# A planner of TensorE's order that charges for changes between wide, full and tiled matmuls

## The chip, the cores and the metric

One core of a Trainium2 chip runs the whole kernel. The metric is the device time of one execution in microseconds, median of several runs; the profile is one further execution, of which every instruction is recorded. TensorE (PE) does the matmuls, VectorE (DVE), ScalarE (ACT) and GpSimd (POOL) the rest, and SyncE (SP) issues most of the DMAs.

## What is computed

Two layers of an encoder on 512 tokens of width 1024. Each layer normalises, projects to 3728 columns, runs four token mixers on parts of them, joins them in an output projection, and then routes each of 16 experts to its 64 best tokens. Cut from the reference:

```
for l in range(DEPTH):                                   # DEPTH = 2
    h = rms_norm(x, norm_mix_g[l])
    p = jnp.einsum('bsd,dp->bsp', h, w_in[l])
    fa, fb, fc, fd = jnp.split(p, [A_IN, A_IN + B_IN, A_IN + B_IN + C_IN], axis=-1)
    ya = rwkv7_mixer(fa, ...)            # a scan over the tokens, both ways, 4 heads of 64
    yb = gqa_axial_mixer(fb, ...)        # softmax attention, 4 query heads
    yc = gated_deltanet_mixer(fc, ...)   # chunks of 64 tokens, both ways, 4 heads
    yd = dilated_window_mixer(fd, rel_bias)              # windowed attention, 6 heads
    x = x + jnp.einsum('bsm,md->bsd', jnp.concatenate([ya, yb, yc, yd], -1), w_out[l])
    x = x + expert_choice_ffn(rms_norm(x, norm_ffn_g[l]), ...)   # 16 experts x 64 tokens, 3 weights of 1024x1024 each
return rms_norm(x, norm_final_g)
```

## The kernel before, in words

A layer has two stages. In the **mixers' stage** the projection (L701, and L838 for the output) runs as triples of fp32r matmuls over the full array, 128 rows by 128 columns, 512 wide: a high and a low half of the weights and of the activations. These are the wide matmuls. Mixers A and C work in heads of 64, and so in matmuls on a quarter of the array (64 rows by 64 columns, which the profile writes 64\*64), in a long chain of small steps through TensorE and VectorE: Gram matrices (L1130, L1381), a blockwise inverse (L912, L917), a solve (L942, L960), a scan of 8 chunks (L981, L988 in `scan`), the output (L1016, L1209), a transpose at the end (L1232 for A, L1440 for C). Each runs twice in a layer, for two groups of heads; tiles of A's chain are called cA, those of C's cC. Mixers B (L1493, L1505, L1515) and D (L1560, L1569, L1579) are attention, in matmuls of 64 rows by 128 columns and of 128 rows by 64, with transposes on the full array between. In the **experts' stage** 402 MB of weights in both layers flow through 17 slots of 1 MB on SyncE's queue (L1805), and L1819 multiplies with them, 128 rows by 64 columns. A router, a top-64 on VectorE (L1679, L1680) and a gather come before the first expert.

No engine's order is written by hand. The class `Order` records every instruction as the program is built, groups matmuls that were written one after the other into nodes of up to 700 ns by its own costs, and plans: `forward` is a list scheduler that goes through time, and whenever an engine is free takes the ready node of highest rank; `backward` makes new ranks from the plan. After six rounds (`ROUNDS`) the plan with the earliest end by the planner's own clock is kept, and every engine's order is fixed by it. So a change of TensorE's choices also moves the orders of the other engines. Only TensorE has a chooser of its own, `pick` (L240): it takes the node of highest rank, except that it takes a dense one if little dense work was done in the last `WINDOW`, or a thin one if much was (`LOW`, `HIGH`). A heap's entry is the pair of minus the rank and the number, ranks are in ns, so an entry's first number within 5000 of another's means 5 us of rank. A matmul costs the same there whatever stood before it:

```
i = self.pick(heaps[e], t) if e == "PE" else heapq.heappop(heaps[e])[1]
start[i] = t
end = free[e] = t + nodes[i]["cost"]
```

## Time and profile before

| | us |
|---|---|
| median of 3 runs (2005.76 to 2012.01) | 2007.81 |
| the profiled execution, its own time | 2007.23 |
| its span, first to last instruction | 2005.4 |
| PE busy in the span | 1748.3 (87%) |
| DVE busy | 977.4 (49%) |
| ACT busy, POOL busy | 442.0, 348.1 |
| DMA | 471.95 MB, mean 235 GB/s |

Beside the mean shares the profile has the span cut in stretches: of each engine the time that it was busy there, the clock that TensorE was granted as a share of 2.4 GHz, and the rate of the DMAs. The mixers' stages are about 0 to 509 us and 998 to 1493 us, the experts' 509 to 998 and 1493 to 1985. In the timeline each row has the start, the duration, the engine, the line, what is written from what, the array's rows and columns with the shapes, and after the x how many records were merged. A matmul in plain fp32 leaves two records, one in fp32r or a transpose leaves one. The recorded ends of matmuls are modelled and overlap the next one, so what a matmul costs is read from its start to the next one's start.

### The profile page before, as it was taken

Reading aid. Unit: us, or ns where it says so; the run is one execution under the profiler, and the core shown is the slowest. Engines: PE = TensorE matmul, PEld = TensorE weight load, DVE = VectorE, ACT = ScalarE, POOL = GpSimd, SP = SyncE. Lnnn points to the kernel's source line nnn. Section 1 sums busy time; section 2 is a strip of 40 time slices with the busy share of each in tenths; the row PEclk is TensorE's granted clock in tenths of the full one; section 3 lists DMA queues with packets and bytes.
Section 4 is the critical chain, followed back from the end, with each engine's and each line's share of the span. In section 5 each row is a group of like instructions: output and inputs, shape, how many; then the busy total and the mean of one; then the engine's idle time right before and its main releaser. Section 6 shows DMA issues by size and latency. Waiting matters only on the chain. (4 is left out here: it accounts for less than half of the span.)

```text
span 2005.4 us, 31717 instructions
## 1 busy us (share of the span) xinstructions
PE 1748.3 (87%) x12870; PEld 957.5 (48%) x12870; DVE 977.4 (49%) x2581; ACT 442.0 (22%) x882; POOL 348.1 (17%) x313
## 2 busy tenths in 40 slices
PE   6989999999499988869889999999877998798695
PEld 5766666666233322323267666667652332232232
DVE  5597878667422212222166977785872222221223
ACT  4333343433001000000034333334320000000001
POOL 3452124320100000000054511433101000000000
PEclk9999999999699998989989899999988999999898
DMA  5311111226799999999842111112297999999995
GB/s 143 79 36 28 38 35 38 64 71 261 285 409 409 409 409 408 409 409 409 346 141 66 27 33 35 39 33 88 86 361 297 408 409 409 409 409 409 409 409 239
DMA packets 191797, 471.95 MB, mean 235 GB/s; under 512 B 24411, under 2 KB 82683, under 8 KB 191522
## 3 DMA queue, kind: packets, MB, share of 16 engines
q1 hardware_dynamic: 186037, 457.07, 60.2%
q0 software_dynamic: 2816, 8.53, 1.1%
q10 hardware_dynamic: 2797, 4.32, 0.6%
q8 instruction: 101, 1.65, 0.3%
q14 instruction: 46, 0.38, 0.1%
HBM read 461.40 MB, written 8.48 MB: 234 GB/s over the span
## 5 line engine op out<-in xcount | busy, mean ns | idle before, releaser
L1819 PE MATMUL bd<-we,xh 128*64 128x512 f32 x800 | 210.7, 606 | 33.5 <-DMA we<-in_expert_w_up_dram 33.5
L1819 PE MATMUL cA<-we,xh 128*64 128x512 f32 x768 | 191.6, 596 | 22.7 <-DMA we<-in_expert_w_down_dram 22.7
L487 POOL TENSOR_TENSOR wl<-wr,wh 128x512 fp32r<-128x512 f32 x104 | 143.1, 1377 | 349.2 <-PE pj L701 262.0
L1819 PE MATMUL pj<-we,xh 128*64 128x512 f32 x800 | 203.1, 604 | 0.1
L701 PE MATMUL pj<-hh,wh 128*128 128x512 f32 x336 | 153.6, 457 | 0.0
L487 DVE TENSOR_TENSOR y<-cA,y 128x512 fp32r<-128x512 f32 x32 | 22.1, 692 | 268.5 <-ACT y L1750 268.3
L1819 PEld LDWEIGHTS bd<-we,xh 128*64 128x64 f32 x800 | 64.6, 139 | 161.8 <-issue 105.9
L1708 POOL DMA_INDIRECT xh<-xg,idx x16 | 15.5, 971 | 706.8 <-DVE idx L1705 437.5
L701 PE MATMUL pj<-hh,wl 128*128 128x512 f32 x336 | 133.3, 397 | 0.0
L701 PE MATMUL pj<-hl,wh 128*128 128x512 f32 x336 | 133.2, 397 | 0.0
L1819 PEld LDWEIGHTS cA<-we,xh 128*64 128x64 f32 x768 | 59.5, 137 | 139.2 <-issue 96.7
L1819 PEld LDWEIGHTS pj<-we,xh 128*64 128x64 f32 x800 | 60.2, 138 | 108.4 <-issue 101.8
L504 DVE SCALAR_TENSOR_TENSOR xh<-xh,gate,bd 128x512 f32<-128x512 f32 x32 | 23.9, 747 | 173.5 <-PE bd L1819 171.6
L1819 PE MATMUL bd<-slab,xh 128*64 128x512 f32 x224 | 72.6, 623 | 37.5 <-DMA slab<-in_expert_w_up_dram 37.5
L838 PE MATMUL pj<-slab,b 128*128 128x512 f32 x320 | 98.5, 423 | 3.6 <-DVE xres L487 1.5
L504 DVE SCALAR_TENSOR_TENSOR xh<-xh,pj 128x512 f32<-128x512 f32 x34 | 23.4, 687 | 155.1 <-ACT xh L507 155.1
L507 ACT ACTIVATE xh<-pj 128x512 f32<-128x512 f32 x46 | 27.4, 596 | 308.3 <-PE pj L1819 304.6
L669 ACT CAST wh<-wr 128x512 fp32r<-128x512 f32 x104 | 63.9, 617 | 87.1 <-PE pj L701 40.8
L1819 PE MATMUL cA<-slab,xh 128*64 128x512 f32 x256 | 76.4, 598 | 7.3 <-DMA slab<-in_expert_w_down_dram 7.3
L701 PEld LDWEIGHTS pj<-hh,wh 128*128 128x128 f32 x336 | 64.3, 191 | 31.8 <-issue 18.2
L1750 ACT CAST y<-cA 128x512 fp32r<-128x512 f32 x32 | 18.7, 585 | 247.8 <-PE cA L1819 247.8
L701 PEld LDWEIGHTS pj<-hh,wl 128*128 128x128 f32 x336 | 63.8, 190 | 14.8
(473 smaller groups left out, 3207.5 us busy)
## 6 DMA issues: line engine op xcount, KB each, us to landing
we<-in_expert_w_gate_dram SPq DMA_DIRECT2D x100, 1024.0 KB
we<-in_expert_w_up_dram SPq DMA_DIRECT2D x98, 1024.0 KB
we<-in_expert_w_down_dram SPq DMA_DIRECT2D x96, 1024.0 KB
slab<-in_expert_w_down_dram SPq DMA_DIRECT2D x32, 1024.0 KB
slab<-in_expert_w_up_dram SPq DMA_DIRECT2D x28, 1024.0 KB
slab<-in_expert_w_gate_dram SPq DMA_DIRECT2D x28, 1024.0 KB
wr<-in_w_in_dram SPq DMA_DIRECT2D x96, 256.0 KB
b<-in_w_out_dram SPq DMA_DIRECT2D x20, 256.0 KB
```

What stands on the lines that cost most here:

```text
L487: (eng or self.nc.vector).tensor_tensor(out, a, b, op=op)
L504: (eng or self.nc.vector).scalar_tensor_tensor(out, a, s, b, op0=op0, op1=op1)
L507: self.nc.scalar.activation(out, a, fn, **k)
L669: nc.scalar.copy(hi, w)
L701: self.nc.tensor.matmul(pt[:, sl], a[:, k % 4], b[:, k, sl], start=(k == 0 and i == 0), stop=(k == KC - 1 and i == 2))
L838: nc.tensor.matmul(pt, a, b, start=(i == 0), stop=(i == len(terms) - 1))
L1708: nc.gpsimd.indirect_dma_start(dst, None, src, bass.IndirectOffsetOnAxis(ap=idx, axis=0))
L1750: nc.scalar.copy(yh[:, f], pts[f])
L1819: self.nc.tensor.matmul(pts[f][sl], src[:, kk, sl], w[ei][k][:, 512 * f : 512 * f + 512], start=(kk == 0), stop=(kk == KC - 1))
```

## The change

The planner gets three numbers: `STAY` = 5000, `LONG` = 2600, `TURN` = 160 (ns). `record` gives every matmul a kind: "dense" if its operands are not plain fp32 (the wide ones), "tiled" if it is plain fp32 and uses less than 128 rows or 128 columns, "plain" otherwise (mostly transposes). A node keeps the kind of its first and of its last matmul. `pick` first looks for ready nodes that begin with the kind that TensorE is at, and whose rank is within `STAY` of the best; as long as less than `LONG` was spent in that kind, the best of these is taken, ahead of the old rules for dense and thin work. A node of another kind costs `TURN` more on the planner's clock. No instruction is added or taken away; orders alone change. Below the planner every line number of the changed kernel is 12 higher than before (L701 is L713 there).

```diff
+    STAY, LONG, TURN = 5000.0, 2600.0, 160.0
...
+            kind = "dense" if not f32 else "tiled" if k[1] - k[0] < 128 or o[1] - o[0] < 128 else "plain"
...
             node = last
+            node["out"] = kind
...
+            if eng == "PE":
+                node["in"] = node["out"] = kind
...
-        if done < self.LOW and rate(top) < self.DENSE:
+        alike = [e for e in heap if nodes[e[1]]["in"] == self.state and e[0] < top[0] + self.STAY]
+        if alike and self.stay < self.LONG:
+            top = min(alike)
+        elif done < self.LOW and rate(top) < self.DENSE:
...
-        rec.append((t + nodes[i]["cost"], nodes[i]["work"]))
-        return i
+        turn = 0.0 if nodes[i]["in"] == self.state else self.TURN
+        self.stay = 0.0 if turn else self.stay + nodes[i]["cost"]
+        self.state = nodes[i]["out"]
+        self.turns += turn > 0
+        rec.append((t + turn + nodes[i]["cost"], nodes[i]["work"]))
+        return i, turn
...
-                    i = self.pick(heaps[e], t) if e == "PE" else heapq.heappop(heaps[e])[1]
+                    i, turn = self.pick(heaps[e], t) if e == "PE" else (heapq.heappop(heaps[e])[1], 0.0)
                     start[i] = t
-                    end = free[e] = t + nodes[i]["cost"]
+                    end = free[e] = t + turn + nodes[i]["cost"]
```

Counted over both orders, in the mixers' stages of the two layers: neighbours of different kind fall from 716 to 410. Neighbours of different array shape (128\*128, 64\*64, 128\*64, 64\*128 and a few smaller ones) fall from 698 (347 and 351) to 512 (257 and 255). Of the 716, 177 are between plain and dense, both on the full array; afterwards 101. Changes between one tiled shape and another, which are of one kind for the planner, rise from 163 to 205. In the experts' stages changes of shape fall from 121 to 93.

The first place is TensorE in the first layer, where the solve of A's first group (L942, four blocks of 8) runs between projections (L701) and B's attention. Before:

```order
L1493 MATMUL bd_2776<-xh_2194,xh_2193 128x512
L942 MATMUL cA_969<-g_115_701,ar_566 64x64 x8
L942 MATMUL cA_970<-g_115_701,ar_566 64x64 x8
L942 MATMUL cA_969<-g_115_701,ar_566 64x64 x8
L701 MATMUL pj_2730<-hh_103,wh_2725 128x512
L701 MATMUL pj_2730<-hl_104,wh_2725 128x512
L701 MATMUL pj_2730<-hh_103,wl_2726 128x512
L701 MATMUL pj_2730<-hh_103,wh_2725 128x512
L701 MATMUL pj_2730<-hl_104,wh_2725 128x512
L701 MATMUL pj_2730<-hh_103,wl_2726 128x512
L942 MATMUL cA_970<-g_115_701,ar_566 64x64 x8
L1505 MATMUL bd_2787<-const,ba_2782 128x128 x4
```

and with the change (L942 is L954, L701 is L713, L1493 is L1505):

```order
L1505 MATMUL bd_2776<-xh_2194,xh_2193 128x512
L954 MATMUL cA_969<-g_115_701,ar_566 64x64 x8
L954 MATMUL cA_970<-g_115_701,ar_566 64x64 x8
L954 MATMUL cA_969<-g_115_701,ar_566 64x64 x8
L954 MATMUL cA_970<-g_115_701,ar_566 64x64 x8
L713 MATMUL pj_2644<-hh_103,wh_2633 128x512
L713 MATMUL pj_2644<-hl_104,wh_2633 128x512
L713 MATMUL pj_2644<-hh_103,wl_2634 128x512
L713 MATMUL pj_2644<-hh_103,wh_2633 128x512
L713 MATMUL pj_2644<-hl_104,wh_2633 128x512
L713 MATMUL pj_2644<-hh_103,wl_2634 128x512
```

The solve's four blocks stand together, where a projection stood between the third and the fourth.

The second place is TensorE in the first layer's second scans, of A (cA) and C (cC) at once; L838 is the output projection of the rows of mixers that are ready. Before:

```order
L988 MATMUL cA_3683<-g_624_3313,g_619_3293 64x64
L988 MATMUL cA_3684<-g_624_3313,g_619_3293 64x64
L988 MATMUL cA_3683<-g_624_3313,g_619_3293 64x64
L988 MATMUL cA_3684<-g_624_3313,g_619_3293 64x64
L838 MATMUL pj_5169<-slab_4939,b_945_5165 128x512 x2
L838 MATMUL pj_5169<-slab_4939,ba_5166 128x512
L1569 MATMUL bd_5210<-const,ba_5199 128x128 x2
L981 MATMUL cA_3701<-g_655_3655,g_634_3374 64x64
L981 MATMUL cA_3702<-g_655_3655,g_634_3374 64x64
L981 MATMUL cA_3701<-g_655_3655,g_634_3374 64x64
L981 MATMUL cA_3702<-g_655_3655,g_634_3374 64x64
L988 MATMUL cC_4279<-g_751_4193,g_738_4060 64x64
```

and with the change (L981 is L993, L988 is L1000, L1569 is L1581, L1579 is L1591, L1560 is L1572):

```order
L1000 MATMUL cA_3683<-g_624_3313,g_619_3293 64x64
L1000 MATMUL cA_3684<-g_624_3313,g_619_3293 64x64
L1000 MATMUL cA_3683<-g_624_3313,g_619_3293 64x64
L1000 MATMUL cA_3684<-g_624_3313,g_619_3293 64x64
L1581 MATMUL bd_5252<-const,ba_5241 128x128 x2
L1000 MATMUL cC_4279<-g_751_4193,g_738_4060 64x64
L1000 MATMUL cC_4278<-g_751_4193,g_738_4060 64x64
L1000 MATMUL cC_4279<-g_751_4193,g_738_4060 64x64
L1000 MATMUL cC_4278<-g_751_4193,g_738_4060 64x64
L993 MATMUL cA_3701<-g_655_3655,g_634_3374 64x64
L993 MATMUL cA_3702<-g_655_3655,g_634_3374 64x64
L993 MATMUL cA_3701<-g_655_3655,g_634_3374 64x64
```

Between the first and the last step of these two scans there are 42 matmuls of L838 before in either layer, and none afterwards; they stand ahead of the scans or behind them.

The third place is TensorE at the head of A's first chain in the second layer: four matmuls of L1085 give the decays and rates that A's work on ACT and VectorE starts from. Before:

```order
L1085 MATMUL cA_8150<-xh_7944,lw_8109 128x512
L701 MATMUL pj_9839<-hh_7767,wh_9826 128x512
L701 MATMUL pj_9839<-hl_7768,wh_9826 128x512
L701 MATMUL pj_9839<-hh_7767,wl_9827 128x512
L701 MATMUL pj_9839<-hh_7767,wh_9826 128x512
L701 MATMUL pj_9839<-hl_7768,wh_9826 128x512
L701 MATMUL pj_9839<-hh_7767,wl_9827 128x512
L1085 MATMUL cA_8155<-xh_7944,lw_8109 128x512
L1085 MATMUL cA_8156<-xh_7944,lw_8109 128x512
```

and with the change (L1085 is L1097, L1023 is L1035):

```order
L713 MATMUL bd_9908<-hh_7767,wl_9898 128x512
L1097 MATMUL cA_8150<-xh_7944,lw_8109 128x512
L1097 MATMUL cA_8155<-xh_7944,lw_8109 128x512
L1035 MATMUL pj_9866<-const,b_1826_9864 128x2 x4
L713 MATMUL cC_7824<-hh_7767,g_1498_7776 128x256
L713 MATMUL cC_7824<-hl_7768,g_1498_7776 128x256
L713 MATMUL cC_7824<-hh_7767,g_1499_7777 128x256
L713 MATMUL cC_7824<-hh_7767,g_1498_7776 128x256
L713 MATMUL cC_7824<-hl_7768,g_1498_7776 128x256
```

Before, 9 projection matmuls (L701) stand between the first and the second of the four, 6 between the second and the third, none between the last two. Now it is 18, none and 24.

## Rows read from the trace of the kernel before

**Rows 1.** The page's second part: GB/s that the DMAs moved, in 40 equal slices

```profile
GB/s 143 79 36 28 38 35 38 64 71 261 285 409 409 409 409 408 409 409 409 346 141 66 27 33 35 39 33 88 86 361 297 408 409 409 409 409 409 409 409 239
```

**Rows 2.** Stretches, each stage: us, busy us (instructions) of each engine, granted clock, DMA, GB/s

```profile
0.00:508.90 508.90, 459.27 (x4637) 333.27 (x4637) 369.68 (x1087) 186.95 (x390) 151.01 (x133) 0.96 0.28 84
508.90:998.00 489.10, 413.23 (x1784) 146.31 (x1786) 109.75 (x201) 31.66 (x47) 18.02 (x26) 0.95 0.99 394
998.00:1493.40 495.40, 456.15 (x4645) 328.29 (x4641) 372.27 (x1058) 183.90 (x386) 157.09 (x128) 0.97 0.27 83
```

**Rows 3.** Stretches, the same columns: the mixers' stages without their heads and ends

```profile
50.00:500.00 450.00, 419.42 (x4371) 302.58 (x4370) 336.87 (x983) 162.30 (x344) 133.24 (x111) 0.97 0.24 71
1050.00:1490.00 440.00, 412.53 (x4403) 296.39 (x4401) 338.82 (x986) 163.24 (x348) 131.20 (x110) 0.98 0.24 75
```

**Rows 4.** SyncE's timeline and a stretch: the weights' queue after the mixers of layer one

```profile
548.03 7.29 SPq L1805 DMA_DIRECT2D we<-in_expert_w_gate_dram  x5
...
523.00:545.00 22.00, 13.54 (x49) 5.22 (x51) 3.62 (x10) 1.15 (x1) 5.28 (x9) 0.67 0.37 136
```

**Rows 5.** TensorE's timeline, 418 to 422 us: start us, duration us, what, records

```profile
418.00 0.69 PE L960 MATMUL cC<-g,g 64*64 64x64 f32 x32
418.52 0.30 PE L988 MATMUL cA<-g,g 64*64 64x64 f32 x8
418.64 0.41 PE L960 MATMUL cC<-g,g 64*64 64x64 f32 x16
418.98 0.73 PE L838 MATMUL pj<-slab,b 128*128 128x512 f32 x2
419.55 0.39 PE L838 MATMUL pj<-slab,ba 128*128 128x512 f32 x1
419.78 0.63 PE L838 MATMUL pj<-slab,b 128*128 128x512 f32 x2
...
420.94 0.40 PE L838 MATMUL pj<-slab,ba 128*128 128x512 f32 x1
421.26 0.34 PE L981 MATMUL cA<-g,g 64*64 64x64 f32 x8
421.43 0.41 PE L960 MATMUL cC<-g,g 64*64 64x64 f32 x16
421.77 0.44 PE L1579 MATMUL bd<-ba,dv 128*64 128x128 f32 x4
```

**Rows 6.** TensorE's timeline: transposes on the full array among wide matmuls

```profile
489.06 0.60 PE L636 MATMUL cC<-const,xres 128*128 128x128 f32 x4
489.41 0.95 PE L838 MATMUL pj<-slab,b 128*128 128x512 f32 x3
490.19 0.60 PE L636 MATMUL cA<-const,xres 128*128 128x128 f32 x4
```

**Rows 7.** TensorE's timeline: steps of the second scans in layer one

```profile
427.84 0.34 PE L981 MATMUL cA<-g,g 64*64 64x64 f32 x8
...
430.55 0.34 PE L981 MATMUL cA<-g,g 64*64 64x64 f32 x8
...
450.04 0.28 PE L981 MATMUL cC<-g,g 64*64 64x64 f32 x5
```

**Rows 8.** Stretch, the same columns: the second scans in layer one

```profile
418.00:451.00 33.00, 29.02 (x480) 20.63 (x483) 25.57 (x97) 10.56 (x28) 7.92 (x8) 1.00 0.20 63
```

**Rows 9.** Timeline and a stretch: the head of A's first chain in layer two

```profile
1088.47 1.12 PE L1085 MATMUL cA<-xh,lw 64*128 64x512 f32 x2
...
1094.67 1.13 PE L1085 MATMUL cA<-xh,lw 64*128 64x512 f32 x4
...
1100.00:1150.00 50.00, 43.44 (x362) 31.73 (x360) 49.83 (x148) 18.30 (x34) 26.50 (x21) 0.90 0.12 31
```

**Rows 10.** Stretches: two with the clock that TensorE was granted

```profile
459.00:466.00 7.00, 4.44 (x64) 3.31 (x58) 6.76 (x20) 3.16 (x6) 0.00 (x0) 1.00 0.61 188
462.00:472.00 10.00, 7.24 (x33) 5.22 (x29) 8.86 (x24) 3.08 (x6) 0.00 (x0) 0.83 0.94 322
```

More of the change, by code (lines that the diff above doesn't have):

```diff
@@ L372, in forward @@
         N = len(nodes)
-        self.recent = deque()
+        self.recent, self.state, self.stay, self.turns = deque(), None, 0.0, 0
         need = [len(nd["deps"]) + len(nd["tiles"]) for nd in nodes]
```

## The prediction

> **What bounds the kernel now.** First the rate of the DMAs over the span [rows 1]: near 35 GB/s in most of the mixers' stages, at a flat 409 in the experts' ones. Then the same cut by stages [rows 2]: 508.9 us of mixers with PE busy for 459.3, 489.1 us of experts at 394 GB/s with PE busy for 413.2, and 495.4 us of mixers again with PE busy for 456.2. So the experts' stages belong to the queue of weights, and the mixers' stages to TensorE, most of all in their middle: of 450 us in the first layer PE was busy for 419.4, of 440 in the second for 412.5 [rows 3]. It waited there for 30.6 and 27.5 us, 58 together; DVE comes next with 336.9 and 338.8 us.
>
> A gain in the mixers reaches the end of the kernel. The queue of weights fills its free slots, then stands still until the first experts give slots back: from 523 to 545 us it moved 136 GB/s with PE at work for 13.5 of 22 us, and issues go on at 548 [rows 4]. The first expert starts a fixed chain (router, top 64, gather) after the last matmul of the mixers. If that comes 10 us earlier, so does the stream's second part, as long as the first part is loaded by then, and the 22 us of low rate are the reserve for that. So I pass on what the mixers gain in full, in either layer, and count nothing for the 28 changes of shape that the experts' stages lose: PE waits for weights there.
>
> **What a change costs, from rows.** All in [rows 5], start to start. A wide matmul among its like takes 0.23 us (419.55 to 419.78). The two at 418.98 that follow tiled ones take 0.57, where two would take 0.46: 0.11 more. The wide one at 420.94 that stands before a tiled one takes 0.32: 0.09 more. On the tiled side, 32 records of L960 followed by another 64\*64 group take 0.52, so 16 take 0.26; the 16 at 418.64 that are followed by a wide matmul take 0.34: 0.08 more. There and back is 0.28 us, and the first tiled matmul after the change may add a few hundredths, which these rows don't resolve: 0.14 to 0.17 us a change. I take 0.15.
>
> Two things differ from what the planner charges. **Plain beside dense is free.** Four transposes between triples of wide matmuls take 0.35 us, the triple behind them 0.78 instead of 0.69 [rows 6]: 0.44 for the detour, 0.11 a transpose. If a transpose alone took as long as a quarter of a wide matmul, 0.06, the detour would hold 0.2 us of change, 0.1 each way, and the 76 changes of this kind that go (177 to 101) would save another 7.6 us; nothing in the array's shape changes there, so I take 0 and keep the 7.6 us for the range. **A change between tiled shapes is not free.** The 16 records at 421.43 are followed by L1579 in 128\*64, and take 0.34 [rows 5], as the ones before a wide matmul do. For the planner that is one kind. So shapes are to be counted, not kinds.
>
> The Trainium skill has this as a rule (TensorEngine Tiling (Array Packing), Key Properties): changing the tiling mode, not just the tile, drains the engine. By the rule the sum is one over shapes, as in the row; by the planner's kinds it would be 306 changes and 46 us. The trace sides with the rule against the planner's grouping.
>
> **The sum.** In the mixers 698 changes of shape become 512: 186 less, 90 in the first layer and 96 in the second. At 0.15 us that is 27.9 us less for TensorE, 26 to 32 by the bounds, 39 with the transposes. That is all the change removes; nothing is added, no instruction, no DMA. SyncE's queue keeps its rows, only their places shift with the plan, and the weights' order is fixed by the program. The solve (first place of the order) is a clean case: two changes less, and A's chain gets its fourth block earlier.
>
> **What the longer stays cost.** The second place is where I expect part of the gain to be lost. The second scans have steps of PE, DVE, PE, DVE that can't overlap in one chain. In 418 to 451 us PE was busy for 29.0 of 33 us, DVE for 25.6 [rows 8], and PE was so busy because 42 wide matmuls, 42 x 0.23 = 9.7 us, filled the gaps. They are gone from there. With them go 17 changes of shape, 2.6 us. Of the 31.5 us from the first L988 at 418.52 [rows 5] to the last L981 at 450.04 [rows 7], some 17 us of PE's work stay, with PE's few waits. But the chain has its own pace: a step took 2.71 us where it went fast (427.84 to 430.55, [rows 7]), with DVE serving both chains. Eight steps are 21.7 us. So PE will wait for about 5 us in this scan, and as much in the second layer's, whose order has the same 42 and 0. Bounds: 0, if D's attention and DVE's lighter load let the steps run faster than any seen, and 10 us per layer, if they keep nearly the pace of before (27 of 31.5 us). I take 5, two layers 10.
>
> A wait like this can cost the clock. TensorE was busy for 4.4 of 7 us from 459 to 466, and the mean clock in 462 to 472 is 0.83 [rows 10], that is a third of the stretch at 1.2 instead of 2.4 GHz: some 3.4 us, worth up to 1.7 us of wide matmuls. If each second scan brings one such drop, that is 0 to 3.4 us; it lies in the range and not in the sum.
>
> The third place costs in the second layer only. The four L1085 start within 6.2 us before (1088.47 to 1094.67, [rows 9]); with 42 projection matmuls among them instead of 15 the fourth comes 27 x 0.23 = 6.2 us later, less where the 256-wide ones take half: about 5. Behind it is the one stretch where DVE is the bound, 49.8 of 50 us [rows 9]. DVE can do other work meanwhile; 0 to 5 us, I take 2.
>
> Sum: -27.9 + 10 + 2 = -15.9. From the profiled execution's 2007.2 that gives 1991.3; that execution lies 0.6 below the median, which I leave aside: **1991 us**.
>
> **Rivals.**
>
> *The gain arrives whole, or more.* The planner had a TensorE without changes, so every plan ran late by 698 x 0.15 = 105 us, and the orders of DVE and ACT were made for times that never came. With a price close to the measured one they fit better, and some of the 58 us of waiting goes too. Without losses in the scans: 1979; with 8 us of waiting gone as well: 1971. Against it: the price is put on kinds, so 101 changes are still charged that cost nothing and 205 are not charged that do.
>
> *It gives back what it saves.* Fillers taken out of the second scans cost 20 us by the upper bound above, the head 5, a clock drop in each layer 3: 28 of 28, so 2007. The range of this case is 1999 to 2013.
>
> *Slower: stays ahead of the chains.* A stay may last 2.6 us on the planner's clock while a better-ranked chain matmul waits. A layer goes through two rounds of A and C in series, each some 30 hops from PE to DVE and back; 60 hops a layer, 120 in all. One wide matmul more ahead of each hop, 0.23 us, is 28 us: there it turns. At two it is 28 us slower, 2035. For it: between the first and last step of C's first scan in layer one there are 75 projection matmuls where there were 51, 5.5 us more. Against it: in the three other first scans the count goes 45 to 42, 39 to 45 and 54 to 54, and the inverse and solve stand closer together than before. Range 2013 to 2035.
>
> *The change doesn't do what it says* I can leave out: the order shows it.
>
> **How the numbers follow.** A measurement of this kernel tells about 0.3%, 6 us, from no change: faster is below 2001.8, slower above 2013.8. Part given back, 1983 to 1999: 0.45. Whole or more, 1970 to 1983: 0.17. Given back, 1999 to 2013: 0.20, a quarter of it below 2001.8. Slower: 0.18. So faster 0.45 + 0.17 + 0.05 = 0.67, same 0.15, slower 0.18. The range leaves out 0.05 below 1974 and 0.14 above 2016, so it is 1974 to 2016; the forecast's own is 1983 to 1999.
>
> **What would show it.** PE's busy time in the mixers should fall by about 28 us over both layers, and the first wide matmul after tiled ones be as dear as before, only rarer. In the second scans no L838, a span of 20 to 24 us instead of 31.5, and waits of PE for DVE of some 5 us that weren't there. The stretches at 409 GB/s should be as long as before and start earlier, by about 7 us in the first layer and 16 in the second. The fourth L1085 of layer two should start later after the first. I am wrong if PE's waits in the mixers grow by more than 28 us, if the clock falls in many places, or if the gap in the weights' queue closes before the mixers' gain is spent. The place that decides is the second scan: if its steps take 3.5 us although nothing fills them, the gain is gone.

## The result and the profile with the change

The change makes the kernel slower: 2021.04 us, median of five runs (2015.92 to 2026.88), against 2008.98 for the kernel before beside it. The ratio is 1.0063, 95% interval 1.0045 to 1.0082. The forecast was 1991 us with a range to 2016; the time is outside it, on the other side. The profiled execution of the change took 2015.92 us, the fastest of its five; its span is 2014.1.

The page with the change, the granted clock and the rate of the DMAs in 40 slices (the rate answers [rows 1]):

```profile
PEclk9979999989699998989989799999888999999898
GB/s 147 80 30 18 39 51 38 85 45 186 353 409 409 409 409 409 409 409 409 344 130 74 19 28 40 44 27 96 44 323 351 409 408 409 410 408 410 409 409 239
```

The granted clock of before in the same slices:

```profile
PEclk9999999999699998989989899999988999999898
```

Stretches of the trace with the change, columns as in [rows 2]: the stages, then the mixers without head and end, which answer [rows 3]:

```profile
0.00:509.00 509.00, 449.58 (x4637) 339.48 (x4637) 366.09 (x1087) 187.42 (x390) 148.01 (x133) 0.94 0.25 76
1001.00:1498.00 497.00, 447.65 (x4643) 337.10 (x4639) 362.79 (x1057) 183.61 (x386) 152.10 (x128) 0.94 0.25 74
...
50.00:500.00 450.00, 408.95 (x4355) 307.02 (x4356) 331.22 (x977) 160.90 (x341) 129.58 (x111) 0.94 0.21 61
1050.00:1490.00 440.00, 403.57 (x4352) 303.94 (x4350) 325.38 (x960) 160.88 (x342) 127.17 (x111) 0.95 0.21 62
```

PE's busy time fell by some 10 us in the first layer and 9 in the second, not by 14 each. It waits in the middle of the mixers for 41.1 and 36.4 us instead of 30.6 and 27.5 [rows 3], and its granted clock there is 0.94 and 0.95 instead of 0.97 and 0.98. So each of the two things that should have stayed small grew.

From both traces I took the start of the last router transpose (L1674 of before), of the first expert matmul (L1819) and of the last L1756 of each layer. All later tables use these. "Half clock" is the time at a granted clock of 0.5, "waits" the idle time ahead of matmuls inside the stage, "changes" the neighbours of different array shape in the order. All in us, first layer + second layer:

| | before | with the change |
|---|---|---|
| mixers, to the last L1674 | 508.2 + 488.1 | 508.6 + 489.9 |
| from there to the first L1819 (top 64, gather) | 26.0 + 25.6 | 29.1 + 28.9 |
| experts, to the last L1756 | 470.7 + 469.7 | 470.0 + 470.5 |
| sum | 1988.2 | 1997.0 |
| half clock in the mixers | 38.7 + 30.7 | 57.9 + 60.5 |
| waits in the mixers | 48.3 + 37.9 | 58.4 + 48.2 |
| changes in the mixers | 347 + 351 | 257 + 255 |

The mixers gain nothing although 186 changes are gone, and the gather, which nobody touched, loses 6.4 us. The table holds one execution of each kernel, with the change the fastest of its five: these two differ by 8.7 us, the medians by 12.1.

**The gather.** The weights' queue and the first gather in the first layer, with the change (SyncE's timeline; SyncE's waits from 455 to 500; VectorE's wait for the gathered rows; a stretch that answers [rows 4], and the time of the gather itself):

```profile
471.79 26.51 SPq L1817 DMA_DIRECT2D we<-in_expert_w_gate_dram  x8
...
SPq L1817 <- PE cC L1028: 15.6, 1, 15.6
...
534.47 0.31 DVE L513 TENSOR_SCALAR gate<-gs 64x1 f32<-64x1 f32 x2 [8.79 <-DMA gs<-ag,idx]
...
523.00:545.00 22.00, 10.06 (x39) 4.22 (x41) 3.72 (x10) 1.47 (x2) 3.40 (x7) 0.63 0.71 280
526.00:536.00 10.00, 0.27 (x2) 0.27 (x2) 0.30 (x2) 1.15 (x1) 2.12 (x2) 0.50 1.03 411
```

The same of before, for rows that were not shown:

```profile
SPq L1805 <- PE cC L1016: 1.4, 1, 1.4
...
462.30 0.89 SPq L1805 DMA_DIRECT2D we<-in_expert_w_gate_dram  x2
...
530.98 0.31 DVE L501 TENSOR_SCALAR gate<-gs 64x1 f32<-64x1 f32 x2 [5.72 <-DMA gs<-ag,idx]
526.00:536.00 10.00, 3.75 (x14) 2.19 (x16) 1.68 (x4) 1.15 (x1) 2.11 (x2) 0.50 0.20 57
```

The prefetch waits for C's last output matmul of the layer (L1028, L1016 before), which comes 9.5 us later, so it starts 9.5 us later and still runs at 411 GB/s when the gather starts. The gather waits 3.1 us longer, and everything behind it too.

**The second scans.** Stretches from the first L988 to the last L981 of the second scans, with the change and before ([rows 7] end there), in the first layer also the stretch from there to the last L1674:

```profile
430.10:456.70 26.60, 23.62 (x373) 17.93 (x374) 22.55 (x101) 11.34 (x25) 5.29 (x5) 0.68 0.20 61
456.70:508.60 51.90, 45.15 (x424) 35.15 (x420) 40.69 (x149) 14.02 (x32) 1.09 (x3) 0.97 0.56 212
1417.50:1444.00 26.50, 23.55 (x373) 17.76 (x374) 22.31 (x101) 11.47 (x25) 5.27 (x5) 0.68 0.19 62
```

```profile
418.50:450.10 31.60, 28.08 (x455) 19.83 (x446) 24.95 (x93) 9.81 (x26) 7.76 (x7) 1.00 0.19 61
450.10:508.20 58.10, 50.30 (x437) 37.26 (x431) 44.60 (x170) 19.15 (x44) 1.12 (x3) 0.96 0.72 270
```

No L838 is left, as the order says. But the scan takes 26.6 us, not 20 to 24. PE waits for 3.0 us there, not for more than the 3.5 of before. What is new is the clock: 0.68, which is 17.1 us at 1.2 GHz in a stretch that had full clock before.

The 42 matmuls of L838 all stand ahead of these scans now: between the first and the second scans there are 96 of them in either layer instead of 54, behind the second ones 120 as before. So the second scans start later (11.6 us in the first layer), and the stretch behind them is no longer than before, 51.9 us instead of 58.1.

### The profile page after: what moved, and what is told of

It is laid out like the page before. It is cut to its first block, busy times and chain, and to the rows that moved or that the text cites. A ratio compares the mean times of both kernels' runs of the same rounds, so it can differ in the third digit from the quotient of the medians.

```text
span 2014.1 us, 31694 instructions
## 1 busy us (share of the span) xinstructions
PE 1728.0 (86%) x12870; PEld 975.3 (48%) x12870; DVE 961.8 (48%) x2581; ACT 442.3 (22%) x882; POOL 340.2 (17%) x313
## 4 chain that ended last, share of the span: by engine, by line
PE 48%; DMA 23%; DVE 19%; ACT 2%; issue 2%; POOL 1%; SPq 0%; ACTq 0%; DVEq 0%; POOLq 0%
PE pj L1831 8%; DMA we<-in_expert_w_up_dram 8%; DMA we<-in_expert_w_down_dram 7%; PE bd L1831 7%; PE pj L713 7%; PE cA L1831 6%; PE pj L850 4%; DMA slab<-in_expert_w_up_dram 4%; DVE g L499 3%; PE bd L713 1%; PE bd L1505 1%; PE cC L1768 1%; DMA we<-in_expert_w_gate_dram 1%; PE cA L1768 1%; DVE xres L499 1%
## 5 line engine op out<-in xcount | busy, mean ns | idle before, releaser
L713 PE MATMUL pj<-hh,wh 128*128 128x512 f32 x336 | 144.2, 429 | 0.6 <-ACT dv L1550 0.6
L713 PE MATMUL pj<-hl,wh 128*128 128x512 f32 x336 | 134.4, 400 | 0.0
L713 PE MATMUL pj<-hh,wl 128*128 128x512 f32 x336 | 134.2, 399 | 0.0
L516 DVE SCALAR_TENSOR_TENSOR xh<-xh,gate,bd 128x512 f32<-128x512 f32 x32 | 23.9, 747 | 167.7 <-PE bd L1831 165.8
L850 PE MATMUL pj<-slab,b 128*128 128x512 f32 x320 | 92.8, 409 | 6.8 <-ACT b L843 6.2
L1720 POOL DMA_INDIRECT xh<-xg,idx x16 | 15.6, 972 | 418.3 <-PE pj L1831 245.4
L713 PEld LDWEIGHTS pj<-hh,wh 128*128 128x128 f32 x336 | 64.7, 192 | 26.8 <-issue 11.8
L713 PEld LDWEIGHTS pj<-hh,wl 128*128 128x128 f32 x336 | 64.8, 193 | 14.8
```

The source lines that it names most:

```text
L516: (eng or self.nc.vector).scalar_tensor_tensor(out, a, s, b, op0=op0, op1=op1)
L713: self.nc.tensor.matmul(pt[:, sl], a[:, k % 4], b[:, k, sl], start=(k == 0 and i == 0), stop=(k == KC - 1 and i == 2))
L850: nc.tensor.matmul(pt, a, b, start=(i == 0), stop=(i == len(terms) - 1))
L1720: nc.gpsimd.indirect_dma_start(dst, None, src, bass.IndirectOffsetOnAxis(ap=idx, axis=0))
```

## The experiments

### Which part of the change costs

The charge alone, without the preference:

```diff
-        alike = [e for e in heap if nodes[e[1]]["in"] == self.state and e[0] < top[0] + self.STAY]
-        if alike and self.stay < self.LONG:
-            top = min(alike)
-        elif done < self.LOW and rate(top) < self.DENSE:
+        if done < self.LOW and rate(top) < self.DENSE:
```

> The planner charges the 160 ns for a change of kind, but the preference for the same kind in the choice of TensorE's next node is taken out. In its order the changes of array shape in the mixers are 381 and 363 (before 347 and 351, with the change 257 and 255), and no wide matmul stands in the second scans, as with the change. Theory stays (the loss comes from the longer stays, which hold up the chains): time as before, 2003 to 2012 us, waits of TensorE in the mixers as before, about 115 us over both layers. Theory price (the charge alone moves the plan, the fillers out of the second scans with it): no gain from fewer changes and still the loss, 2015 to 2030, with a stretch of some 17 us at half clock in each second scan.

Measured: 2085.23 us, ratio 1.0373 (1.0344 to 1.0402). The charge alone costs 76 us, six times what the whole change costs.

The preference alone:

```diff
-    STAY, LONG, TURN = 5000.0, 2600.0, 160.0
+    STAY, LONG, TURN = 5000.0, 2600.0, 0.0
...
-        self.stay = 0.0 if turn else self.stay + nodes[i]["cost"]
+        self.stay = 0.0 if nodes[i]["in"] != self.state else self.stay + nodes[i]["cost"]
```

> The preference for the same kind stays, the charge is 0. Changes of shape in the mixers 267 and 258, almost as with the change (257 and 255); 9 wide matmuls in each second scan instead of 0 (before 42). Theory stays: as with the change, 2015 to 2025 us. Theory price: the 173 changes fewer than before bring at 0.12 us each about 20 us, and most of it arrives, 1990 to 2003.

Measured: 2005.58 us, ratio 0.9987 (0.9972 to 1.0002), between the two theories. In its profile the mixers are 12.9 us shorter than before; the gather gives back 6.3. So the stays alone do not make the kernel slower. They are not free either: 173 changes fewer are worth 33 us by the fit further down, of which the mixers keep 12.9. The waits, where my rival "stays ahead of the chains" would show with 28 us, grow by 5.

The old rules first, and the preference only where they are silent; then a shorter reach of the preference:

```diff
+        best = top
...
-        if alike and self.stay < self.LONG:
+        if alike and self.stay < self.LONG and top is best:
```

> The old rules for dense and thin work decide first, and the preference for the same kind only where they leave the choice alone. Changes of shape 286 and 279, 133 fewer than before. The stage of the Gram matrices in A's first chain has 45 and 54 wide matmuls in it (before 48 and 48, with the change 24 and 24); the second scans have 3. Theory clock (stretches of tiled matmuls without wide ones fall to 1.2 GHz and that eats the gain): the time at half clock in the mixers falls from some 119 us with the change to at most 80, waits fall too, and the time is 1998 to 2008. Theory stays: the chains are held up as with the change, 2010 to 2022.

```diff
-    STAY, LONG, TURN = 5000.0, 2600.0, 160.0
+    STAY, LONG, TURN = 1000.0, 2600.0, 160.0
```

> Only nodes whose rank is within 1000 instead of 5000 of the best may be preferred for their kind. Changes of shape 294 and 291, 113 fewer than before. A chain's node is held up by less. Theory stays: C's first scan in the first layer has 63 wide matmuls instead of 75, the last transposes of C come earlier than with the change, the weights' first transfer after the mixers starts before 468 us instead of at 471.8, the gather is free of weights, and the time is 1998 to 2008. Theory clock: Gram stage with 21 wide matmuls, second scans with none, so half clock as with the change, about 119 us in the mixers, and 2010 to 2022.

Measured: 2051.61 (1.0205, 1.0180 to 1.0229) and 2034.56 (1.0131, 1.0097 to 1.0166). All four expectations are missed: the less of the preference stands beside the charge, the slower. Half clock in the mixers came to 167 and 146 us, more than with the change, so letting the old rules decide first does not keep the clock.

Those rules count dense work in a window of the planner's time, and the charge stretches that time. So the window was put on a clock without the charges, for the charge alone and for the whole change:

```diff
-        while rec and rec[0][0] < t - self.WINDOW:
+        while rec and rec[0][0] < t - self.lost - self.WINDOW:
...
-        rec.append((t + turn + nodes[i]["cost"], nodes[i]["work"]))
+        rec.append((t - self.lost + nodes[i]["cost"], nodes[i]["work"]))
+        self.lost += turn
```

> As the run with the charge alone, but the window of the old rule for dense and thin work (3413 ns, less than 5000 of dense work in it: take a dense node) is kept on a clock without the charges. In its order the second scans have 51 and 42 wide matmuls again (before 42 and 42, charge alone 0 and 0); changes of shape 367 and 355. Theory rule (the charge stretches the planner's time, the rule finds too little dense work in its window and puts dense nodes ahead of the chains): most of the 76 us comes back, 2005 to 2035. Theory charge itself (a later plan gives bad orders on the other engines): 2065 to 2090 as with the charge alone.

> The change, with the window of the old rule kept on a clock without the charges. Changes of shape 258 and 260, 0 wide matmuls in the second scans as with the change. Theory rule (the loss of the charge comes through that rule): the time falls to that of the preference alone, 1998 to 2010. Theory charge itself: as the change, 2014 to 2028.

Measured: 2069.49 (1.0290, 1.0255 to 1.0326) and 2025.54 (1.0065, 1.0045 to 1.0085). Both go with the theory of the charge itself. Through that rule come some 16 of the 76 us; why the charged plans are worse beyond that stays open. One thing in the code was not tried: `backward`, which makes the ranks, does not charge the changes that `forward` charges.

### What a stage of mixers is made of

Sixteen of the traces are of kernels with the same instructions in the mixers (all but the block of constants and the three with groups done twice). That gives 32 stages. A least-squares fit, one constant for each layer, gives

length = constant + 0.19 x changes + 0.37 x half clock + waits

with standard errors of 0.009 us a change and 0.025 us per us, and 2.4 us of scatter of one stage. With the factor of the waits left free it is 1.05 (0.13). Sums over both layers, us:

| | changes | half clock | waits | mixers | to L1819 | median |
|---|---|---|---|---|---|---|
| before | 698 | 69 | 86 | 996.3 | 51.6 | 2008.98 |
| with the change | 512 | 118 | 107 | 998.5 | 58.0 | 2021.04 |
| charge alone | 744 | 176 | 102 | 1070.2 | 56.5 | 2085.23 |
| charge alone, window corrected | 722 | 108 | 112 | 1052.5 | 51.4 | 2069.49 |
| preference alone | 525 | 96 | 91 | 983.4 | 57.9 | 2005.58 |
| preference by shape | 471 | 113 | 97 | 988.5 | 54.3 | 2002.14 |
| second scans emptied | 680 | 159 | 100 | 1041.2 | 51.8 | 2045.94 |

For the change: 186 x 0.19 = 35.3 us less for changes, 48.9 x 0.37 = 18.1 more for the clock, 20.4 more of waits: 3.2 us longer, where the trace has 2.2. With the gather's 6.4 that is 9.6, where the two profiled executions differ by 8.7. For the charge alone: 8.7 + 39.5 + 15.6 = 63.8 of its 73.9.

The price of half clock can be set beside the Trainium skill (TensorE: Matmul & The Clock Gate, HAM oscillation — how this bites in real kernels), which takes half of the throttled time as the loss. The stages show less, 0.37. In them TensorE stood idle for 15% of the time at half clock, and half of the other 85% would be 0.42, an estimate; the rest of the difference is not explained.

### The price of a change by itself

Blocks of matmuls on constants, put behind the end of the kernel before:

```diff
+        for n, group in ((80, (wide,)), (96, (wide,)), (96, (quarter,)), (80, (wide,)), (96, (wide, quarter)), ...
+            for i in range(n):
+                for g in group:
+                    g()
```

> The kernel before, and behind its end, on constants, blocks of matmuls whose results nobody reads: 96 wide ones (128 rows by 128 columns, 512 wide, fp32r) in a row; 96 groups of eight 64*64 ones in plain fp32 in a row; the same 96 and 96 in turn, so with 192 changes of shape; 96 transposes, and 96 wide and 96 transposes in turn; 48 groups of eight 128*64 ones, in turn with 48 groups of 64*64, and with 48 wide ones. Its time is longer by the blocks and says nothing else. Theory of the prediction: 0.15 us a change (0.14 to 0.17), none between wide and transpose, and as much between 64*64 and 128*64 as to the full array. Theory of the accounting over the runs so far (20 mixers' stages: length less waits against changes and half clock): 0.2 us a change. Theory clock: in the row of 768 tiled matmuls without a wait the granted clock falls to half. Rival: it stays full there, and it is the waits between that let it fall.

TensorE's timeline, in turn: 64\*64 alone, the first records of two groups of 16; 80 wide ones and 96 transposes in rows of their own; 768 records of 128\*64; then pieces of the mixed blocks, wide with 64\*64 (the first record of a group shown), 64\*64 with 128\*64, wide with 128\*64, wide with transposes:

```profile
2029.77 0.22 PE L1802 MATMUL cA<-const 64*64 64x64 f32 x1
...
2030.01 0.22 PE L1802 MATMUL cA<-const 64*64 64x64 f32 x1
...
2166.58 18.43 PE L1796 MATMUL pj<-pa 128*128 128x512 f32 x80
2184.85 10.64 PE L1797 MATMUL bd<-const 128*128 128x128 f32 x96
2195.25 18.66 PE L1796 MATMUL pj<-pa 128*128 128x512 f32 x81
...
2265.05 22.62 PE L1807 MATMUL bd<-const 128*64 128x64 f32 x768
2287.60 18.43 PE L1796 MATMUL pj<-pa 128*128 128x512 f32 x80
...
2099.62 0.51 PE L1796 MATMUL pj<-pa 128*128 128x512 f32 x1
2100.05 0.27 PE L1802 MATMUL cA<-const 64*64 64x64 f32 x1
...
2100.45 0.51 PE L1796 MATMUL pj<-pa 128*128 128x512 f32 x1
...
2320.05 0.27 PE L1802 MATMUL cA<-const 64*64 64x64 f32 x1
...
2320.45 0.69 PE L1807 MATMUL bd<-const 128*64 128x64 f32 x16
2321.06 0.27 PE L1802 MATMUL cA<-const 64*64 64x64 f32 x1
...
2399.67 0.50 PE L1796 MATMUL pj<-pa 128*128 128x512 f32 x1
2400.10 0.69 PE L1807 MATMUL bd<-const 128*64 128x64 f32 x16
2400.72 0.50 PE L1796 MATMUL pj<-pa 128*128 128x512 f32 x1
...
2229.72 0.48 PE L1796 MATMUL pj<-pa 128*128 128x512 f32 x1
2230.04 0.27 PE L1797 MATMUL bd<-const 128*128 128x128 f32 x1
2230.06 0.48 PE L1796 MATMUL pj<-pa 128*128 128x512 f32 x1
```

Alone a wide one takes 18.27 / 80 = 0.228 us, sixteen records of 128\*64 take 22.55 / 48 = 0.470, a transpose 10.40 / 96 = 0.108, sixteen records of 64\*64 0.24 (2029.77 to 2030.01, outside the pauses that this row has, see the last section). A wide one and a 64\*64 group in turn take 0.83 (2099.62 to 2100.45), so a change costs (0.83 - 0.228 - 0.24) / 2 = 0.18. With 128\*64 it is (1.05 - 0.228 - 0.470) / 2 = 0.18. Between 64\*64 and 128\*64 groups the period is 1.01 (2320.05 to 2321.06), so 0.15. Wide and transpose take 0.34 against 0.336: nothing. So the theory of the prediction is right in kind and a little low, the 0.12 of two later expectations lower still, and the fit's 0.19 is near. The Trainium skill's rule (TensorEngine Tiling (Array Packing), Key Properties: a change of tiling mode drains the engine) agrees in all four: time is lost where the shape changes and none where it does not.

The row of 64\*64 groups alone, and the mixed block, as stretches:

```profile
2029.60:2069.00 39.40, 24.87 (x1537) 23.49 (x1536) 0.00 (x0) 0.00 (x0) 0.00 (x0) 1.00 0.02 5
2087.70:2166.60 78.90, 78.90 (x1633) 48.77 (x1632) 0.00 (x0) 0.00 (x0) 0.00 (x0) 1.00 0.01 3
```

Quarter-array work without a wide matmul kept its full clock for 39 us, so the theory "tiled matmuls alone let the clock fall" falls. Nor do waits alone tell the two apart, as the rival had it: this row stood idle for 14.5 of 39.4 us at full clock, the second scans with the change for 3.0 of 26.6, and there the clock fell. They differ also in their records, 1536 in 39 us here and 373 in 26.6 there. What decides is not shown by this run.

### The second scans alone, and the clock as cause

The plan of before is kept; in a last pass no L838 may be taken while a second scan runs. So the order is that of before up to the scans:

```diff
+        if any(0 < len(a) < len(b) for a, b in zip(self.left, self.group)):
+            heap = sorted(e for e in whole if not self.nodes[e[1]]["out838"])
...
+        best = self.forward(best["rank"])
```

> The order of before up to the second scans of each layer, on every engine; while a second scan runs no L838 may be taken, and the rest is planned on from there. So the second place of the change alone: 0 wide matmuls in the second scans instead of 42, 9 changes of shape fewer in each layer. Theory of the prediction: the scans take 20 to 24 us instead of 31.5 with some 5 us of waiting more in each, the clock stays, the 42 come behind; 2003 to 2012 in all. Theory clock: waits of TensorE in the scans as before (3.5 us), but 14 to 17 us at half clock in each, which cost 6 us a layer, so the scans take 26 to 27 us and the whole gets longer by about 8: 2014 to 2020.

Measured: 2045.94 us, ratio 1.0163 (1.0118 to 1.0209), by the ratio 33 us, far above both forecasts for the whole. This is not what the place costs in the change: here the 42 matmuls stand behind the scans (162 instead of 120), in the change ahead of them. What the run has in common with the change is a second scan without them. Then the same order, with each group of the second scans done once more behind itself:

```diff
+        for out, a, b in group:
+            x = self.nc.tensor.matmul(out, a, b, start=True, stop=True)
+            self.order.nodes[-1]["insts"].append(x.ins)
```

> The order of the run with the emptied second scans, on every engine; in the second scans every group of four L988 or L981 is done once more right behind itself, into the same places, so nothing changes but that TensorE has 112 matmuls more in each layer, 5.7 us at full clock by the blocks of constants (49 ns each... 0.051 us). Theory clock: the stretches of some 21 us at half clock in the scans get shorter than 10 us, the scans take 20 to 25 us instead of 27, and the whole is faster than the emptied one by 4 to 20 us, 2026 to 2042. Theory order (the chain or the later L838 make the loss): the scans take 29 to 33 us and the whole 2046 to 2060.

> The order of the change on every engine, with the groups of the second scans done twice in the same way. Theory clock: the 17 us at half clock in each second scan get shorter than 8 us, the scans take 21 to 25 us instead of 26.6, and the whole 2010 to 2019. Theory order: scans of 29 to 32 us, the whole 2024 to 2035.

Stretches: two pieces of the emptied scans where the clock fell, these scans as a whole and the rest to the last L1674, then the same two with the groups done twice, then the scans of the change with the groups done twice:

```profile
424.00:430.00 6.00, 5.25 (x117) 3.93 (x110) 5.44 (x27) 1.86 (x6) 0.20 (x1) 0.92 0.01 4
430.00:436.00 6.00, 5.56 (x74) 3.81 (x74) 5.03 (x26) 1.13 (x5) 0.00 (x0) 0.50 0.01 3
...
423.90:450.90 27.00, 25.16 (x400) 18.98 (x393) 18.10 (x86) 5.64 (x21) 0.20 (x1) 0.60 0.01 3
450.90:531.50 80.60, 66.33 (x485) 48.20 (x480) 52.24 (x175) 24.27 (x49) 9.68 (x9) 0.86 0.71 276
```

```profile
414.00:435.70 21.70, 20.20 (x620) 16.35 (x612) 17.48 (x86) 5.39 (x20) 0.20 (x1) 1.00 0.02 5
435.70:515.50 79.80, 64.91 (x495) 47.12 (x487) 52.69 (x175) 24.43 (x51) 9.32 (x9) 0.89 0.72 277
```

```profile
431.40:458.90 27.50, 25.27 (x588) 20.12 (x591) 22.59 (x101) 11.30 (x25) 5.26 (x5) 0.81 0.20 60
```

Emptied, the scan takes 27 us with 21.9 at half clock and only 1.8 of waiting (the second layer's 26.7, 20.5 and 1.8). With 112 matmuls more it takes 21.7 us in both layers, at full clock, with 1.5 of waiting. Nothing else was changed, and more work in the same order made the scan 5 us shorter, so the clock is the cause of its length. With 3.4 us for the 112 matmuls (0.03 each, 0.24 / 8 by the block), an estimate, half clock cost (27.0 - 21.7 + 3.4) / 21.9 = 0.40 of its time here, near the fit's 0.37. That 21.7 is also the forecast of the scan to the tenth is luck: it holds 112 matmuls that the forecast had not. The whole is 2033.01 us (1.0132, 1.0094 to 1.0169), lower as expected, though the two intervals overlap: the traces of the scans carry this reading, not the totals. Most of the emptied kernel's loss lies behind the scans: 80.6 us instead of 58.1. The 42 moved matmuls are 9.7 of the 22.5, half clock that grows from 4.6 to 22.6 us some 6.7, waits that grow from 6.8 to 13.3 another 6.5.

The fillers and the clock go together over the plans. In the second scans of the sixteen kernels of the fit there are 0 to 6.8 us at half clock with 42 to 51 wide matmuls between the steps, 10.2 to 17.1 with 30 to 33, 10.2 and 13.7 with 9, and 17.1 to 23.9 with 3 or none.

On the order of the change the same trick brings the half clock only from 17.1 to 10.2 us a scan; the scan takes 27.5 and the whole 2024.49 (1.0082, 1.0056 to 1.0108), no better than the change. The scan's time misses both forecasts, the whole lies just inside that of the theory of the order: the 112 matmuls are 3.4 us a layer, the clock regained is 6.9 x 0.37 = 2.6. So for the change itself the clock of the scans is measured, but no run gives its price back.

### The gather

```diff
+            held = len(self.order.queue) - 6
...
+            self.order.queue.insert(held, nc.sync.dma_start(seen, rows[0]).ins)
```

> The order of the change on every engine, and the same instructions. Added is one small DMA ahead of the last four weights of each layer's prefetch (the last three slabs and the two that come after the router, 4.9 MB) on the weights' queue: it reads the result of the first gather, so these weights start when the gather is done. Theory collision (the gather takes 3.1 us longer in each layer because the prefetch, which starts 9.5 us later with the change, still runs at 409 GB/s): from the last L1674 to the first L1819 (lines of before) 26 us instead of 29.1 and 28.9, and 5 to 7 us less than the change in all, 2012 to 2018. Theory of a later gather for another reason: 29 us as with the change, or the held weights come late for the experts, and the time is that of the change or more, 2019 to 2028.

Measured: the way from L1674 to L1819 is 25.9 and 25.7 us, so it is the weights that slow the gather: VectorE waits for its rows as briefly as before.

```profile
541.70 0.31 DVE L516 TENSOR_SCALAR gate<-gs 64x1 f32<-64x1 f32 x2 [5.59 <-DMA gs<-ag,idx]
```

But the experts' stages take 475.7 and 475.6 us instead of 470.0 and 470.5, and the whole 2028.82 (1.0075, 1.0050 to 1.0099), just above the range of the second theory. A stretch of the first layer while the weights are held:

```profile
533.00:543.00 10.00, 0.83 (x2) 0.32 (x2) 2.04 (x7) 1.76 (x2) 3.11 (x6) 0.50 0.21 65
```

The queue stands nearly still for 10 us, and the held 5.2 MB (not the 4.9 of the expectation) are 13 us at 409 GB/s that the experts' stage then has to fetch. Collision shown, remedy not: the gather was sped up by as much as expected, and the stream that bounds the next stage paid for it. This run has the orders of the change but for that one DMA, yet its first mixers' stage took 519.0 us with 80.6 at half clock, against 508.6 with 57.9. So two executions of one order can differ by that much.

### How much is the luck of a plan

A hop costs 201 instead of 200 ns in the planner: nothing that matters, but every order is new. For the kernel before, the change, and a preference by array shape without charge:

```diff
-    HOP, SELF = 200.0, 130.0
+    HOP, SELF = 201.0, 130.0
```

> A change without a meaning in the planner of before: a hop from engine to engine costs 201 instead of 200 ns. Every order is planned anew: changes of shape 344 and 348 instead of 347 and 351. Theory: what the runs show comes from the mechanisms named (changes, half clock, waits), and an order with as many changes takes as long, 2003 to 2015. Rival (luck of the plan): plans that differ by nothing that matters differ by as much as before and after do, more than 12 us: outside 1997 to 2021.

> The same meaningless step, 201 instead of 200 ns a hop, in the planner with the change. Changes of shape 264 and 254 instead of 257 and 255; in C's first scan of the first layer 57 wide matmuls instead of 75, in the second layer's 63 instead of 54. Theory: as the change, 2014 to 2028. Rival (luck of the plan): outside that by more than 5 us, on either side.

> The preference by array shape without a charge, planned with 201 instead of 200 ns a hop. Changes of shape 242 and 231 instead of 240 and 231; 33 and 30 wide matmuls in the second scans as there. Theory (the gain comes from the changes saved): 1995 to 2008 us, ratio below 0.999. Rival (luck of that one plan): ratio 1.000 or more.

The preference by array shape (charge 0), as it is, measured once more in more executions, with its second scans done twice, and with a wider reach (STAY 10000):

```diff
-            kind = "dense" if not f32 else "tiled" if k[1] - k[0] < 128 or o[1] - o[0] < 128 else "plain"
+            kind = (64 if k[1] - k[0] <= 64 else 128, 64 if o[1] - o[0] <= 64 else 128)
```

> Preference for the same array shape (rows and columns, 64 or 128 each) instead of the same kind, no charge. Changes of shape 240 and 231, that is 54 fewer than with the preference for kinds alone (267 and 258) and 227 fewer than before; 33 and 30 wide matmuls in the second scans (before 42, preference for kinds 9). Theory: the changes are worth 0.12 us each on TensorE, 6 us less than the preference for kinds, and TensorE's stretches at half clock in the second scans get shorter: 1992 to 2004. Rival: C's first scans have 96 and 93 wide matmuls in them (before 51 and 54), its chain is held up by some 9 us a layer and the later tail takes the gain: 2004 to 2020.

> The order of the preference by array shape, with the groups of the second scans done twice. There the scans hold 33 and 30 wide matmuls and have 10 us at half clock each. Theory clock: half clock in the scans below 4 us, scans of 31 to 33 us as now (5.7 us more work against 4 us of clock): 1998 to 2008. Theory order: 35 to 38 us a scan, 2006 to 2014.

> The kernel of the run with the preference by array shape (first ratio 0.9954), once more with more rounds. If it is faster than before: 0.993 to 0.998 again. If the first ratio was chance: 0.998 to 1.002.

> The same preference, for nodes within 10000 instead of 5000 of the best rank. Changes of shape 228 and 225 instead of 240 and 231; 30 wide matmuls in each second scan. By the accounting 18 changes fewer are 3.6 us, if clock and waits stay: 1993 to 2005, ratio 0.991 to 0.997. Rival: stays that reach further hold up the chains, waits and half clock take it: 2003 to 2020.

| | median | ratio, 95% interval |
|---|---|---|
| before, 201 | 2003.61 | 0.9969 (0.9951 to 0.9987) |
| change, 201 | 2027.10 | 1.0085 (1.0056 to 1.0113) |
| shape | 2002.14 | 0.9954 (0.9931 to 0.9977) |
| shape, again | 2006.19 | 0.9981 (0.9964 to 0.9999) |
| shape, 201 | 2009.02 | 1.0003 (0.9987 to 1.0020) |
| shape, groups twice | 2004.85 | 0.9980 (0.9960 to 1.0000) |
| shape, reach 10000 | 2005.06 | 0.9973 (0.9957 to 0.9989) |

Before and change with 201 come out as their theories had it, and so does the shape plan's first measurement. The shape plan with 201 goes with its rival, its second measurement with "chance"; reach 10000 just misses the range that the accounting gave. With the groups done twice the second scans had 10.2 us at half clock and took 34.2 us in the first layer, none and 29.9 in the second, where without it both had 10.2: the repetition does not hold the clock every time.

A step without meaning moves the time by 0.2 to 0.5%. So the gain of the preference by shape is no more than the luck of a plan, although its mixers are 4 to 11 us shorter than before in each of the five profiles; in the plan with 201 the way to the first L1819 takes 58.1 us in both layers together, in the others 51.6 to 54.8. The loss of the change is more than luck: its three plans with charge and full preference lie at 1.0063, 1.0065 and 1.0085, the two of before at 1 and 0.9969. Over all plans (the emptied order aside) the seven made with the charge lie at 1.0063 to 1.0373, the six made without it at 0.9954 to 1.0003. By these ratios the version with reach 10000 beats both kernels, by 0.27% and 0.9%; the first is no more than another plan of before gained.

## Why the prediction was wrong, point by point

**The gain for the changes: right, a little low.** 186 changes fewer were taken at 0.15 us, 27.9 us. The block shows 0.18 for a change to the full array and 0.15 between tiled shapes, none for the transposes; the fit over the stages 0.19, which makes 35. That shapes and not the planner's kinds count is confirmed.

**The second scans: this step failed, by the clock.** I expected waits of PE to grow by 5 us in each scan and put 0 to 3.4 us for the clock, in the range only and at nothing in the sum, from one short stretch at 0.83 [rows 10]. The runs show the reverse: no wait grows in these scans, and each has 17.1 us at half clock, 6.3 us by the fit, where the scan exceeds the forecast's 21.7 by 4.9. At 1.2 GHz the matmuls of the chain themselves fill the time that I had booked as waits. In the one order where an emptied scan kept full clock, with its groups done twice, it took 21.7. The step's own sum was loose as well: 31.5 less 9.7 and 2.6 is 19.2 with the waits, where I wrote some 17.

**The same term elsewhere: mis-sized.** I looked at two places. Half clock and waits grew over the mixers as a whole, 49 and 20 us, where the sum had 12 of waits and the range 3.4 us for the clock. By the fit the 49 are 18.1 us. Of them 34.2 lie in the two second scans and 32.3 in A's first Gram stages (L1130) of both layers; elsewhere there is less than before. In the first layer this stage holds 24 wide matmuls with the change instead of 48, and its stretch is 36.5 us instead of 29.0:

```profile
119.30:155.80 36.50, 25.44 (x190) 17.07 (x194) 31.92 (x117) 8.43 (x16) 13.90 (x10) 0.64 0.12 31
```

and before:

```profile
119.80:148.80 29.00, 24.87 (x218) 18.36 (x220) 29.00 (x87) 5.35 (x10) 15.06 (x10) 0.88 0.12 30
```

PE waits 13.3 us there instead of 6.3 (2.2 of either just ahead of the stretch), at a granted clock of 0.64 instead of 0.88. The second layer's has the same 24 and 48, 18.2 us at half clock instead of 5.2, and is as long as before. The waits grow in these two stages by 11.4 us and from A's first scans to the end of C's by 9.7; in the second scans, where I had booked 10, they shrink by 1.2. C's first scan of the first layer, with 75 wide matmuls instead of 51, took 41.7 us instead of 28.2, 5.9 of it waits where there were none, a sign that the rival had named.

**The head of A's chain in layer two: about right.** The fourth L1085 comes 11.1 us after the first (1095.4 to 1106.5) where it was 6.2 [rows 9], 4.9 later; I had put 5 for the delay and 2 for its price. The price alone was not measured.

**"What the mixers gain is passed on in full": the reserve was spent from the other side.** I took the 22 us at 136 GB/s [rows 4] as room for an earlier first expert. But the prefetch itself waits for C's last outputs; with those 9.5 us later it ran into the gather, 6.4 us in both layers that no term of the sum had. I had named a closing gap as what would make me wrong, and priced it at nothing. The first expert's matmul came 3.5 and 8.0 us later than before, not earlier; the 7 us that I had promised for the first layer would have been 8.5 by the sum's own terms.

**The rivals.** The time fell into the range of the slower one, but for the most part not by its mechanism: what it names is seen in the 9.7 us of waits in the first scans. The preference, which lets nodes stay ahead, makes the kernel no slower by itself; shorter stays beside the charge are slower still. "A price close to the measured one makes better plans" is refuted outright: the charge alone costs 76 us, of which the accounting puts some 40 on the clock and 16 on waits, and leaves 10 of the mixers' 74 unexplained. What in the charge makes such plans stays open; the old rules' window explains some 16 us of it.

## What to carry to other kernels

Where TensorE waited here in a chain of small steps, unrelated wide matmuls between the steps paid twice: they used the gaps, and with 42 or more of them a scan had at most 6.8 us at half clock, without them 17 or more. So before fillers are taken out of a thin stretch, price it at half clock too, and don't read its busy share as a sign that it is full. A planner's cost made truer in one term need not make truer plans: time the term alone, beside a step that changes nothing.

## What the runs showed of the hardware that I had not expected

The granted clock fell in stretches in which PE looked busy: 25.16 of 27.0 us with 1.8 us of waits, at a mean clock of 0.60, where TensorE had before it been through the solve and output projections at full clock. Repeating the same small matmuls brought it to 1.00 and the stretch from 27.0 to 21.7 us, on another order only from 17.1 us at half clock to 10.2. In the block of constants 39 us of 64\*64 work kept 1.00 although ten pauses stood in it, in which TensorE was idle for 1.3 to 1.7 us and the profile shows nothing waited for. They come some 3.5 us apart, and between the first ones stand 128 matmul records and 128 weight loads each:

```profile
2035.07 0.21 PE L1802 MATMUL cC<-const 64*64 64x64 f32 x1 [1.29 <-issue]
```

What they wait for was not tried. They are absent where wide matmuls stand between, and in the row of 128\*64 matmuls.
